# A hybrid decoder block on one core: taps at the lowest priority, one side queue per slot, LayerNorms moved into the first phase

## The chip, the cores and the metric

The kernel runs on one core of one Trainium2 chip. The metric is the time of one execution in microseconds (us) on the device. Five engines work beside each other, each in its own fixed order of instructions: PE (matrix products; its weight loads are shown as PEld), DVE (vector), ACT (scalar functions), POOL (GpSimd), and SP, which issues the transfers between device memory and SBUF. Engines wait for each other by semaphores.

## The reference

Sequence 2048, width 1024, one layer. An RMS norm with adaLN scale and shift feeds one input projection to nine groups of columns. Two branches read it:

```python
h = _rmsnorm(x, norm_g) * (1.0 + scale) + shift
p = h @ w_in            # c_val, c_gate, c_og, ts (r, k, v, two low-rank parts), r_og, g_conv, g_rwkv
# branch A
u = c_val * sigmoid(c_gate)
u = causal_depthwise_conv(u, width 31) + b
u = silu(layernorm(u)) * silu(c_og)
y_conv = u @ w_conv_out
# branch B, per head of 64, over time t
state = state * w_t - (state @ kk_t) b_t + v_t k_t ; o_t = state @ r_t
o = groupnorm(o) + sum(r * k * r_k) * v
y_rwkv = (o * silu(r_og)) @ w_rwkv_out
# merge
m = sigmoid(g_conv) * y_conv + sigmoid(g_rwkv) * y_rwkv
out = rmsnorm(x + gate * (m @ w_out)) * final_g
```

`shift`, `scale` and `gate` are three column groups of `silu(c) @ ada_w + ada_b`.

## The kernel before

**Precision and products.** Every large product is made of three: the operands are split into a high and a low part, and `mm3` (L183) adds high·high, low·high and high·low for each of eight k tiles, 24 matmuls of 128x128 by 512 columns. `load_w` (L150) brings a weight tile; the input weights are split in block 0 as they are first used and written back as two tiles (`kh_in`, `kl_in`) that later blocks read. Other weights are split ahead by `presplit` (L132), two halves for each of sixteen items of the list `later`, in blocks 1 and 2.

**First phase.** The sequence is cut into four blocks of 512 rows, and each block into four slots (`slot`, L979), one per group of four heads. A slot has 18 products: K, R and V for two pairs of heads, and the list `FILL`: two convolution columns (`c`, two products each) and two of each of the four gates. A convolution column is then 31 taps on DVE (`taps`, L856), each a pass over 128x512 from a PSUM accumulator. A pair of heads is prepared by `pair` (L483). `group` (L627) inverts the triangular blocks (POOL, L653 and L655), then runs eight chunks of 64 rows, each of three steps on PE with DVE between them, then the group norm (L803 to L812), two sets of transposes (L819) and the write of `o`.

**Order.** PE's order is that of the program text: PE is under a manual schedule. The text is interleaved by a small written clock: each matmul product adds to `now`, and tasks (generators) go on when their due time has come. `yield a, b` means that the step just issued took `a` us of PE and the next is due `b` us later. `drain` advances the clock until the named tasks are done; no product is issued meanwhile. A slot begins with a drain of its predecessor's side task and of the group opened two slots earlier; a group starts only when the group before it is done. The order on the other engines, SP's queue too, is set by a planner from priorities and estimated times; `tc.high_priority(n)` moves instructions ahead by n.

**Side work in the slots.** `xnorm` (L350) norms the row tiles of the next block and transposes them. In blocks 1 and 2 `presplit` comes ahead of it. In block 3, `z_first` (L926) and `lnorm_first` (L883) do z and the LayerNorm of block 0. At a block's start `hprep` (L389) loads the normed input and splits it. All these tiles come from one pool tag, `hx`, with seven buffers. The gate column (the third part of `ada_w`) is made after slot 0 of block 0 (L1034).

**Second phase.** For each block: `rproj` (L1094, eight products) into `mr`, `cproj` (L1080, eight products), then the output projection in four column blocks (L1186 to L1188), residual, and the final norm by row tile (`finish`, L1198), one chain of small operations for each. `osplit` (L1065) makes z of the next block from `o`, `bv` and `ro`, and `lnorm` (L1120) its LayerNorm, beside the output projection. `mr` shares its buffers with the outgoing rows `xt`. The last group's recurrence runs beside the first two projections of this phase.

Of the kernel before, what the change touches and what calls it, by code (L numbers as in the profile page):

```python
# [18 lines left out]
P = 128  # L19
# [27 lines left out]
US_MM, US_K = 0.228, 0.684  # L47


XN = ((0,), (1,), (2, 3), ())  # L50
ZN = ((0, 1, 2), (3, 4, 5), (6, 7), ())
# [15 lines left out]
def hybrid_block(ctx: ExitStack, tc: tile.TileContext, x, vecs, convk, w2a2, final_g, ada, w_in, w_co, w_ro, w_o, crow, out,  # L67
# [12 lines left out]
    def scratch(n):  # L80
        return [[dp.tile([P, TB], F32, name=f"{n}{b}_{j}", tag=f"{n}{b}_{j}") for j in range(KT)] for b in range(NB)]

    o_dram, bv_dram, ro_dram, y_dram, co_dram, gc_dram, gr_dram = [
        scratch(n) for n in ("o_d", "bv_d", "ro_d", "y_d", "co_d", "gc_d", "gr_d")]

    z_dram = [dp.tile([P, TB], F32, name=f"z_d{j}", tag=f"z_d{j}") for j in range(KT)]
    u_dram = [dp.tile([P, TB], F32, name=f"u_d{j}", tag=f"u_d{j}") for j in range(KT)]
# [42 lines left out]
    later = [("o", (cb, kh)) for cb in range(4) for kh in range(2)] + [("ro", j) for j in range(KT)]  # L130
# [215 lines left out]

    def hx(name):
        return xp.tile([P, TB], F32, name=name, tag="hx")

    def xnorm(b, tts):  # L350
        for tt in tts:
# [3 lines left out]
            for half in range(2):  # L355
                xt = hx("xt")
                nc.sync.dma_start(xt, x[t0:t0 + P, half * TB:half * TB + TB])
                nc.scalar.activation(hx("xsq"), xt, AF.Square, accum_out=ss[:, half:half + 1])
                xh.append(xt)
            vs, rs = ss[:, 2:3], ss[:, 3:4]  # L360
            nc.vector.tensor_tensor(out=vs, in0=ss[:, 0:1], in1=ss[:, 1:2], op=ALU.add)
            nc.vector.tensor_scalar(out=vs, in0=vs, scalar1=1.0 / D, scalar2=RMS_EPS, op0=ALU.mult, op1=ALU.add)
            rsqrt(rs, vs, e2, nc.vector, ss[:, 4:5])
            for kh in range(2):
                nc.vector.tensor_scalar(out=xh[kh], in0=xh[kh], scalar1=rs, scalar2=None, op0=ALU.mult)
            yield 0.0, 18.0
            for kh in range(2):
# [10 lines left out]
                yield 0.6, 3.5  # L378
# [10 lines left out]
    def hprep(b):  # L389
        h = ([], [])  # L390
        for k in range(KT):
            hf = hx("hf")
            nc.sync.dma_start(hf, xT_dram[b][:, k, :])
            hsplit(h, k, hf)
        return h
# [87 lines left out]
    def pair(G, q_, box):  # L483
# [45 lines left out]
        yield 0.0, 3.0  # L529
# [29 lines left out]
        yield 0.0, 4.5  # L559

        for c4 in range(NCH // 4):
# [13 lines left out]
            yield 1.2, 2.6  # L575
# [38 lines left out]
    def opened(b, g, h, lora):  # L614
        G = Group()
        G.b, G.g, G.h, G.lora, G.tri, G.pairs, G.wait = b, g, h, lora, 0, 0, 0.0
# [10 lines left out]
    def group(G, before):  # L627
# [60 lines left out]
        yield 0.0, 4.5  # L688
# [62 lines left out]
        for c in range(NCH):  # L751
# [11 lines left out]
            yield 0.6, 2.0  # L763
# [16 lines left out]
            yield 1.1, 2.0  # L780
# [8 lines left out]
            yield 0.6, 2.8  # L789
# [13 lines left out]
        nc.vector.tensor_reduce(out=r4(st), in_=O16, axis=AX.X, op=ALU.add)  # L803
        nc.vector.tensor_scalar(out=st, in0=st, scalar1=1.0 / 64, scalar2=None, op0=ALU.mult)
        nc.gpsimd.tensor_tensor(out=O16, in0=O16, in1=bc(st), op=ALU.subtract)
        for half in range(2):
            Dm = lt.tile([P, 8, 64], F32, name="Dm", tag="oc", bufs=OCB)
            nc.scalar.activation(Dm.rearrange("p (a b) n -> p a b n", a=2), O16[:, half * 2:half * 2 + 2], AF.Square)
            nc.vector.tensor_reduce(out=st[:, half * 8:half * 8 + 8], in_=Dm, axis=AX.X, op=ALU.add)
        nc.vector.tensor_scalar(out=st, in0=st, scalar1=1.0 / 64, scalar2=GN_EPS, op0=ALU.mult, op1=ALU.add)  # L810
        rsqrt(rs, st, lt, nc.vector)
        nc.gpsimd.tensor_tensor(out=O16, in0=O16, in1=bc(rs), op=ALU.mult)  # L812
        yield 0.5, 18.0
        for q in range(2):
# [7 lines left out]
            nc.sync.dma_start(o_dram[b][pr], oc)  # L822
            yield 0.6, 2.5
            if "o" in dbg:
                nc.sync.dma_start(dbg["o"][pr, :, b * TB:(b + 1) * TB], oc)
# [30 lines left out]
    def taps(b, j, u, before):  # L856
        if before is not None:
# [3 lines left out]
        nc.vector.tensor_scalar(out=acc, in0=u[:, HALO:], scalar1=ck[:, j, HALO:HALO + 1], scalar2=vc("conv_b", j),  # L861
                                op0=ALU.mult, op1=ALU.add)
        for i in range(HALO):
            if i % 2:
                yield 0.0, 2.0
            nc.vector.scalar_tensor_tensor(out=acc if i + 1 < HALO else yj, in0=u[:, i:i + TB],  # L866
                                           scalar=ck[:, j, i:i + 1], in1=acc, op0=ALU.mult, op1=ALU.add)
# [13 lines left out]
    ln0 = {}  # L881

    def lnorm_first(part):  # L883

        def yload(j):
            yj = hx("lny")
            nc.sync.dma_start(yj, y_dram[0][j])
            return yj

        if part == 0:  # L890
            ys = yload(0)
            for j in range(1, KT):
                nc.gpsimd.tensor_tensor(out=ys, in0=ys, in1=yload(j), op=ALU.add)
            ln0["ys"] = ys
        elif part == 1:
            ps = pl.tile([P, TB], F32, name="late", tag="late")
            nc.tensor.matmul(ps, ones, ln0["ys"], start=True, stop=True)
            ln0["mean"] = ln0["ys"]
            nc.scalar.copy(ln0["mean"], ps)
            for j in range(KT):  # L900
                yj = yload(j)
# [63 lines left out]
    def once(f):  # L965
        yield free
        f()
# [298 lines left out]
```

## Time and profile before

| | |
|---|---|
| median of 3 runs | 3078.06 us (3073.18 to 3084.1) |
| the profiled execution | 3076.14 us, span 3074.4 us |
| PE busy | 2806.0 us, 91% |
| DVE busy | 2092.9 us, 68% |
| POOL busy | 1183.6 us, 38% |
| ACT busy | 1003.0 us, 33% |
| DMA | 666.90 MB, mean 217 GB/s |
| mean granted clock of PE | 0.963 |

A row of the profile's groups names line, engine, operation, tiles written and read, count, busy time, mean duration, and the idle time of the engine just ahead of it. A row of PE's waits gives the total in us, how often, and the longest. Matmuls overlap, so one that is shown with 392 ns starts about 0.23 us after its predecessor.

### The profile page before, as it was taken

How to read it: one execution, taken by the hardware profiler on the slowest of the kernel's cores; microseconds unless marked ns; L12 is line 12 of the kernel's file. 1: busy time of each engine (PE TensorE's matmuls, PEld its weight loads, DVE VectorE, ACT ScalarE, POOL GpSimd, SP SyncE). 2: the span in 40 equal slices, each digit the busy share in tenths (PEclk: the TensorE clock that was granted, in tenths of full speed). 3: DMA queues.
4: the chain of work that ended last, by engine and by line, in shares of the span. 5: the costliest groups of instructions: out<-in, count | busy, mean ns of one | idle time of the engine just before them, and what ended most of it. 6: DMA issues, size and time to landing. Idle time of an engine off the chain costs nothing.

```text
span 3074.4 us, 50973 instructions
## 1 busy us (share of the span) xinstructions
PE 2806.0 (91%) x18640; PEld 2292.0 (75%) x18640; DVE 2092.9 (68%) x4279; ACT 1003.0 (33%) x1932; POOL 1183.6 (38%) x1742
## 2 busy tenths in 40 slices
PE   6879898986999999789999998999999999799998
PEld 5657676765877778577777777778777778588888
DVE  6857676775676766766676678677877645785633
ACT  4324343423332423242333222332423223342411
POOL 3454637343424242324243334454551315652100
PEclk9989999998999999899999999999999999899999
DMA  8775767575666674656566557665664758877665
GB/s 305 271 233 200 233 226 258 199 248 173 194 198 204 194 243 159 209 170 216 176 211 220 185 169 263 208 210 171 227 199 153 256 189 293 305 250 240 217 225 177
DMA packets 354795, 666.90 MB, mean 217 GB/s; under 512 B 134704, under 2 KB 153456, under 8 KB 354544
## 3 DMA queue, kind: packets, MB, share of 16 engines
q1 hardware_dynamic: 354544, 663.64, 64.9%
q8 instruction: 147, 2.41, 0.3%
q14 instruction: 104, 0.85, 0.1%
HBM read 483.07 MB, written 179.31 MB: 215 GB/s over the span
## 4 chain that ended last, share of the span: by engine, by line
PE 40%; DVE 15%; DMA 8%; POOL 6%; issue 4%; SPq 2%; ACT 1%; POOLq 0%; DVEq 0%; ACTq 0%
PE ps_main L180 27%; DVE acc L866 5%; PE pout L1187 2%; PE pout L1186 2%; PE pout L1188 2%; DMA w_st<-w_ro_t 1%; POOL TT L655 1%; POOL itmp L653 1%; PE aux L569 1%; DMA w_gr<-grow_d 1%; PE xo L766 1%; SPq L666 1%; PE xo L740 1%; DVE S L786 1%; PE xo L782 1%
## 5 line engine op out<-in xcount | busy, mean ns | idle before, releaser
L180 PE MATMUL ps_main<-h_hi,w_hi 128*128 128x512 f32 x2304 | 966.3, 419 | 27.1 <-ACT w_hi L163 14.5
L180 PE MATMUL ps_main<-h_hi,w_lo 128*128 128x512 f32 x2304 | 918.9, 399 | 12.4 <-DMA w_lo<-kl_in 4.8
L180 PE MATMUL ps_main<-h_lo,w_hi 128*128 128x512 f32 x2304 | 915.6, 397 | 0.2 <-DVE h_lo L385 0.2
L866 DVE SCALAR_TENSOR_TENSOR acc<-u,ck,acc 128x512 f32<-128x512 f32 x928 | 697.9, 752 | 21.0
L180 PEld LDWEIGHTS ps_main<-h_hi,w_hi 128*128 128x128 f32 x2304 | 442.5, 192 | 121.5 <-ACT w_hi L163 16.4
L180 PEld LDWEIGHTS ps_main<-h_hi,w_lo 128*128 128x128 f32 x2304 | 440.2, 191 | 120.7 <-POOL w_lo L165 7.6
L180 PEld LDWEIGHTS ps_main<-h_lo,w_hi 128*128 128x128 f32 x2304 | 442.7, 192 | 80.1 <-DVE h_lo L385 1.4
L653 POOL TENSOR_TENSOR itmp<-La,TT 128x126 f32<-128x126 f32 (+22 forms) x496 | 181.9, 367 | 156.4 <-DMA La<-dA 120.5
L786 DVE SCALAR_TENSOR_TENSOR S<-xo,pe,Se 64x64 f32<-64x64 f32 x512 | 144.7, 283 | 141.9 <-PE xo L782 129.4
L163 ACT CAST w_hi<-w_st 128x1024 fp32r<-128x1024 f32 x103 | 108.0, 1048 | 307.2 <-DMA w_st<-w_in_t 128.1
L655 POOL TENSOR_TENSOR TT<-TT,itmp 128x126 f32<-128x126 f32 (+22 forms) x496 | 190.9, 385 | 35.3
L165 POOL TENSOR_TENSOR w_lo<-w_st,w_hi 128x1024 fp32r<-128x1024 f32 x50 | 120.5, 2409 | 133.0 <-ACT w_hi L163 58.2
L761 ACT ACTIVATE Se<-S,pe 128x128 f32<-128x128 f32 x256 | 89.0, 395 | 142.9 <-DVE S L786 141.9
L766 PEld LDWEIGHTS xo<-Xz,As 128*64 128x64 f32 x1024 | 69.6, 138 | 70.4 <-DVE Xz L762 38.4
L165 DVE TENSOR_TENSOR w_lo<-w_st,w_hi 128x1024 fp32r<-128x1024 f32 x53 | 70.5, 1331 | 68.0 <-PE ps_main L180 38.3
L572 DVE TENSOR_TENSOR As<-aux,maskA 128x512 f32<-128x512 f32 x128 | 82.7, 684 | 47.5 <-PE aux L569 47.0
L450 ACT ACTIVATE t<-ps_main,mu 128x512 f32<-128x512 f32 x96 | 65.9, 686 | 136.5 <-PE ps_main L180 133.9
L735 ACT COPY Xz<-xo 64x256 f32<-64x256 f32 x128 | 46.9, 367 | 189.4 <-PE xo L740 129.6
L766 PE MATMUL xo<-Xz,As 128*64 128x64 f32 x1024 | 87.4, 229 | 23.2 <-DVE Xz L762 23.0
L777 DVE TENSOR_TENSOR uv<-xo,rn 64x256 f32<-64x256 f32 x128 | 53.7, 419 | 80.3 <-PE xo L766 66.6
L847 POOL COPY u<-tail 128x30 f32<-128x30 f32 x32 | 10.2, 322 | 251.5 <-DVE yj L866 237.7
L762 DVE TENSOR_TENSOR Xz<-xo,Xz 64x256 f32<-64x256 f32 x128 | 53.7, 420 | 77.4 <-PE xo L757 75.8
(296 smaller groups left out, 5531.1 us busy)
## 6 DMA issues: line engine op xcount, KB each, us to landing
w_hi<-kh_in SPq DMA_DIRECT2D x219, 512.0 KB, 3.9
w_lo<-kl_in SPq DMA_DIRECT2D x219, 512.0 KB, 5.1
w_st<-w_in_t SPq DMA_DIRECT2D x73, 512.0 KB, 4.5
kh_in<-w_hi SPq DMA_DIRECT2D x71, 512.0 KB, 2.9
kl_in<-w_lo SPq DMA_DIRECT2D x71, 512.0 KB, 3.5
w_hi<-kh_ro SPq DMA_DIRECT2D x32, 512.0 KB, 4.0
w_lo<-kl_ro SPq DMA_DIRECT2D x32, 512.0 KB, 5.1
w_st<-w_co_t SPq DMA_DIRECT2D x32, 512.0 KB, 3.6
```

The costliest lines, as they stand in the source:

```text
L163: nc.scalar.copy(hi, st)
L165: lo_eng.tensor_tensor(out=lo, in0=st, in1=hi.bitcast(F32), op=ALU.subtract)
L180: nc.tensor.matmul(ps[:, qs], ww[:, k, :], aa[k][:, qs], start=(k == 0 and t == 0 and q == 0), stop=(k == KT - 1 and t == 2 and q == ms - ...
L450: nc.scalar.activation(t1, ps, AF.Identity, scale=mu1[:, mi:mi + 1])
L572: nc.vector.tensor_tensor(out=Asb[:, hh, c4 * 4:c4 * 4 + 4, :].rearrange("p (a e) n -> p a (e n)", e=2), in0=pA[hh], in1=flat(maskA).unsqu ...
L653: nc.gpsimd.tensor_tensor(out=tmp[:, :ni, :nt], in0=La[:, j:j + 1, j + 1:].broadcast_to([P, ni, nt]), in1=TT[:, :ni, j:j + 1].broadcast_to ...
L655: nc.gpsimd.tensor_tensor(out=TT[:, :ni, j + 1:], in0=TT[:, :ni, j + 1:], in1=tmp[:, :ni, :nt], op=ALU.add)
L761: nc.scalar.mul(Se[:, q, :], Sg[:, q, :], R[q]["pe"][:, c:c + 1])
L766: nc.tensor.matmul(b_[pr_, q, hs], As[q][:, hh, c, kcol(e)], Xz[:, e, q, hs], start=(n == 0), stop=(n == 3), skip_group_check=True)
L786: nc.vector.scalar_tensor_tensor(out=Sg[hs, q, hs], in0=b_[hs, 2 + q, hs], scalar=R[q]["pe"][hs, c:c + 1], in1=Se[hs, q, hs], op0=ALU.mult ...
L866: nc.vector.scalar_tensor_tensor(out=acc if i + 1 < HALO else yj, in0=u[:, i:i + TB], scalar=ck[:, j, i:i + 1], in1=acc, op0=ALU.mult, op1 ...
L1186: nc.tensor.matmul(o_, mhi[kk][:, ts_], whi[:, k, :], start=first, stop=False, skip_group_check=True)
```

## The change

1. The taps carry a priority of −1500, below everything else.
2. Each slot has one side task, `sides(b, g)`: the norm of the next block (row tiles 0 and 1 in slot 0, 2 and 3 in slot 1), then the gate column (slot 0 of block 1), then steps of the LayerNorm of block b−1 (slots 1 to 3 of blocks 1 to 3), then the weight splits of blocks 1 and 2. The list `later` has the `ro` weights first.
3. `lnorm_first` is a generator for any of blocks 0 to 2, and the second phase only loads and splits its result. z is made in the tail of each group, by two POOL operations on each pair, instead of in `z_first` and `osplit`. Block 3 keeps `lnorm` in the second phase.
4. The loads of the next block's input are issued ahead of the last three products of a block.
5. Small operations of the block norm and the group norm get a high priority; many due times are longer. The final norm's small operations are one chain for four row tiles, except in the last column block of the last block.

```diff
+LOWP = 1500
-XN = ((0,), (1,), (2, 3), ())
-ZN = ((0, 1, 2), (3, 4, 5), (6, 7), ())
+XN = ((0, 1), (2, 3), (), ())
...
-    later = [("o", (cb, kh)) for cb in range(4) for kh in range(2)] + [("ro", j) for j in range(KT)]
+    later = [("ro", j) for j in range(KT)] + [("o", (cb, kh)) for cb in range(4) for kh in range(2)]
...
     def xnorm(b, tts):
+        held = []
         for tt in tts:
...
-            yield 0.0, 18.0
+            held.append((tt, xh))
+            yield 0.0, 8.0
+        yield 0.0, 28.0
+        for tt, xh in held:
             for kh in range(2):
...
+    def hload(b):
+        hfs = []
+        for k in range(KT):
+            hf = hx("hf") if k < HXB else e1.tile([P, TB], F32, name="hf", tag="sq")
+            nc.sync.dma_start(hf, xT_dram[b][:, k, :])
+            hfs.append(hf)
+        return hfs
...
@@ def pair @@
-        yield 0.0, 3.0
+        yield 0.0, 4.5
-        yield 0.0, 4.5
+        yield 0.0, 6.0
-            yield 1.2, 2.6
+            yield 1.2, 3.0
@@ def group @@
-        yield 0.0, 4.5
+        yield 0.0, 6.0
-            yield 0.6, 2.0
+            yield 0.6, 2.6
-            yield 1.1, 2.0
+            yield 1.1, 2.5
-            yield 0.6, 2.8
+            yield 0.6, 3.3
...
-        yield 0.5, 18.0
+        yield 0.5, 30.0
+        yield lambda: G.gated
         for q in range(2):
...
-            nc.sync.dma_start(o_dram[b][pr], oc)
+            for src, op in ((bv_dram, ALU.add), (ro_dram, ALU.mult)):
+                zt = spare("zt")
+                nc.sync.dma_start(zt, src[b][pr])
+                nc.gpsimd.tensor_tensor(out=oc, in0=oc, in1=zt, op=op)
+            nc.sync.dma_start(z_dram[b][pr], oc)
             yield 0.6, 2.5
...
+            with tc.high_priority(-LOWP):
+                nc.vector.scalar_tensor_tensor(out=acc if i + 1 < HALO else yj, in0=u[:, i:i + TB],
+                                               scalar=ck[:, j, i:i + 1], in1=acc, op0=ALU.mult, op1=ALU.add)
...
+    def sides(b, g):
+        if b + 1 < NB:
+            yield from xnorm(b + 1, XN[g])
+        if b == 1 and g == 0:
+            yield from gate_col()
+        yield from norms(b, g)
+        if b in (1, 2):
+            for _ in range(2):
+                n_ = later.pop(0)
+                for half in range(2):
+                    presplit(*n_, half)
+                    yield 0.0, 4.0
+    def norms(b, g):
+        if b and g >= 1:
+            t = lns.setdefault(b, lnorm_first(b - 1))
+            for _ in range((0, 3, 5, 99)[g]):
+                r = next(t, None)
+                if r is None:
+                    break
+                yield r
...
+        fill(len(todo) - 3)
+        drain(*side)
+        hfs = hload(b + 1)
         fill(len(todo))
+        return hfs
...
-            ohl = osplit(b + 1)
-            uhl = lnorm(b + 1)
+            ohl = lsplit(z_dram[b + 1], okt(b + 1))
+            uhl = lsplit(u_dram[b + 1], utiles()) if b + 2 < NB else lnorm(b + 1)
...
+            def tail_rs(tt, n):
+                vs = f2.tile([P, n], F32, name="vs", tag=f"vs{n}")
+                nc.vector.tensor_reduce(out=vs, in_=sq4[:, tt:tt + n, :], axis=AX.X, op=ALU.add)
+                nc.vector.tensor_scalar(out=vs, in0=vs, scalar1=1.0 / D, scalar2=RMS_EPS, op0=ALU.mult, op1=ALU.add)
+                rs = f2.tile([P, n], F32, name="rs2", tag=f"rs{n}")
+                rsqrt(rs, vs, f2, nc.vector, f2.tile([P, n], F32, name="rs_t", tag=f"rt{n}"))
+                return rs
...
         if b + 1 < NB:
+            rall = tail_rs(0, NTT)
             for tt in range(NTT):
-                finish(tt)
+                finish(tt, rall)
```

`gate_col` makes the gate column from sixteen loads of 128x512 with one DVE operation each, 3 us apart by the written clock. `lnorm_first(b)` loads y three times (for the mean, the variance and the output), does its sums and products on POOL (46 operations), squares and the swish on ACT and DVE, and writes `u_dram[b]`.

245 lines of the change are left out of this document (120 added, 125 removed).

## The prediction

> **What bounds the kernel now.** I read the page first, then the engines by stage, then what TensorE (PE) waited for, then single places.
>
> ```profile
> span 3074.4 us, 50973 instructions
> ...
> PE 2806.0 (91%) x18640; PEld 2292.0 (75%) x18640; DVE 2092.9 (68%) x4279; ACT 1003.0 (33%) x1932; POOL 1183.6 (38%) x1742
> ```
> PE is the bound, and it sits idle for 3074.4 − 2806.0 = 268 us. No edit takes a large matmul away, so the change can only win or lose in those 268 us and in the clock that PE loses behind them. The profiled execution took 3076.14 us, 1.9 us under the median of 3078.06; all sums start from 3076.
>
> The stretches below are blocks 0 to 3 of the first phase, then the first two projections of the second phase, then its middle. Columns: length, busy time of PE, PEld, DVE, ACT, POOL, granted clock, DMA share.
> ```profile
> 0.00:663.00 663.00, 571.87 (x3573) 453.24 (x3573) 478.23 (x963) 259.46 (x447) 322.62 (x433) 0.94 0.71 239
> 663.00:1262.00 599.00, 551.51 (x3882) 446.46 (x3880) 407.08 (x883) 191.17 (x390) 222.31 (x396) 0.97 0.62 199
> 1262.00:1866.00 604.00, 557.36 (x3881) 451.22 (x3880) 417.10 (x893) 190.59 (x390) 202.42 (x380) 0.96 0.60 194
> 1866.00:2437.00 571.00, 544.72 (x3831) 439.89 (x3831) 421.14 (x842) 177.98 (x343) 260.24 (x417) 0.99 0.63 210
> 2437.00:2562.00 125.00, 116.49 (x772) 93.25 (x773) 69.67 (x136) 33.70 (x65) 17.82 (x12) 0.95 0.62 206
> 2617.00:2880.00 263.00, 230.12 (x1139) 192.25 (x1139) 194.52 (x323) 96.56 (x162) 121.46 (x78) 0.94 0.74 254
> ```
> Block 3 already carries a LayerNorm and the z products in its slots, has no norm of a next block, and is the shortest block: 571 us against 599 and 604.
>
> PE's waits (total, times, longest), the rows the sum uses:
> ```profile
> PE late L371 <- DVE xt L365: 49.4, 2, 27.7
> PE xo L766 <- DVE Xz L762: 23.0, 22, 3.0
> PE ps_main L180 <- DVE mr L1100: 18.5, 2, 15.9
> ...
> PE ps_main L180 <- ACT h_hi L384: 12.2, 3, 5.3
> ...
> PE aux L533 <- ACT sq L525: 9.9, 7, 4.7
> ...
> PE aux L569 <- POOL KR L552: 6.8, 5, 2.3
> PE xo L782 <- DVE uv L777: 6.7, 7, 3.7
> ...
> PE ps_main L180 <- DMA w_lo<-kl_in: 4.8, 3, 2.3
> PE aux L589 <- DVE As L572: 4.6, 5, 1.6
> ...
> PE xo L757 <- DVE S L786: 3.9, 5, 1.3
> ...
> PE pmean L1132 <- POOL ys L1130: 2.0, 1, 2.0
> ```
>
> **Price of the clock.** After the 27.7 us wait PE ran like this:
> ```profile
> 716.00:721.00 5.00, 4.93 (x14) 4.10 (x15) 0.32 (x1) 1.51 (x4) 0.00 (x0) 0.50 0.32 105
> ```
> Half clock for 5 us: a long wait costs 5 × 0.5 = 2.5 us on top of itself. I charge that for every long wait that goes or comes.
>
> **The change, part by part.**
>
> *The block norm goes ahead of the weight splits (gain 54).* In blocks 1 and 2, slot 0 first issues four halves of weight splits, and the norm's loads come behind them on SP, in the same seven `hx` buffers:
> ```profile
> 672.79 0.54 SPq L139 DMA_DIRECT2D w_st<-w_o_t  x1
> ...
> 694.42 0.41 SPq L142 DMA_DIRECT2D w_gr<-grow_d  x1
> ...
> 700.70 0.42 SPq L357 DMA_DIRECT2D xt<-x_in  x1
> ...
> 702.09 0.38 SPq L357 DMA_DIRECT2D xt<-x_in  x1
> ```
> The loads go out 28 us after the first split, while the transposes are due after 18 us; PE, whose order is fixed, stands. In the new side queue the norm is first and its transposes are due 8+28 us after the second tile's loads. I take both waits as gone: 49.4 + 2 × 2.5 = 54 (from 0, if another user of `hx` delays them, to 54). Late next would be the splits, on which nothing in the block waits.
>
> *Group norm tail (gain 18).* It rises in priority and gets 30 us instead of 18 before its transposes. In block 0 its wait is the second largest:
> ```profile
> PE late L819 <- POOL uv L812: 17.6, 2, 10.9
> ```
> With two clock losses that is 22.6; I take 18, between 0 and 22.6. Its z products (two POOL operations per pair, two more loads) stand behind the transposes, and PE waits for none of them before the second phase.
>
> *Gate column from block 0 to block 1 (gain 9).* Eight 512 KB loads on SP and eight DVE operations leave block 0, where weights are still being split as they are used; from 140 to 215 us PE waited:
> ```profile
> PE ps_main L180 <- ACT w_hi L163: 14.0, 3, 5.9
> PE ps_main L180 <- POOL w_lo L165: 3.7, 3, 1.4
> ```
> Part of this is block 0's own weight traffic; I take half of 17.7, bounds 0 and 18. In block 1 the same bytes come as sixteen loads spaced by 3 us.
>
> *Loads of the next block's input (gain 12).* They go out three products early instead of at the boundary. Three waits of 12.2 with 7.5 of clock; the split still needs the old block's `h_hi` buffers back, which the last product holds, so I keep 12 of 19.7 (bounds 0, 20).
>
> *Second phase without the LayerNorms of blocks 1 and 2 (gain 28).* The last-named wait of `mr` (15.9) is a queue on DVE: four separate chains of tiny operations, final scale, then `mr`, whose buffer is that of the outgoing `xt`.
> ```profile
> 2621.72 9.95 POOL L1151 TENSOR_TENSOR y<-y,rl 128x512 f32<-128x512 f32 x8 [1.95 <-DVE rs_t L112]
> ...
> 2626.81 1.28 DVE L114 SCALAR_TENSOR_TENSOR rs<-rs_t,rs 128x1 f32<-128x1 f32 x2
> ...
> 2642.22 0.23 DVE L114 SCALAR_TENSOR_TENSOR rs<-rs_t,rs 128x1 f32<-128x1 f32 x2
> ...
> PE ps_main L180 <- DVE w_lo L165: 6.3, 3, 5.7
> ```
> Beside LayerNorm's POOL work two one-column operations took 1.28 us, without it 0.23. One joined chain, and no LayerNorm there, should leave about 2 us of output DMA: 14 + 2.5; the `w_lo` wait goes, 5.7 + 2.5; `pmean` 2.0; the second `mr` wait (18.5 − 15.9 = 2.6) loses 1. Sum 27.7; bounds 8 and 30. Block 3's LayerNorm stays, and so does the end: the last row tiles keep their own small chains.
>
> *Taps lowest, longer due times (gain 20).* The waits for Xz, uv, S, KR, As and sq come to 23.0+6.7+3.9+6.8+4.6+9.9 = 55. Taps no longer stand ahead of those operations on DVE and each step has 0.4 to 1.5 us more cover. How the planner really orders DVE the trace cannot show; between 0 (or below: taps late would hold `u`) and 55 I take 20.
>
> *The price of longer due times: the chain of groups (cost 15).* A group's steps, here in slot 6 of the run, which PE's `pw` row delimits (981.7 to 1121.0):
> ```profile
> L495 PE MATMUL aux<-lw,wl x3: 388/388/477, 981.7 to 1121.0; 128*128 128x512 f32 x3
> ...
> L700 PE MATMUL late<-T,As x32: 191/191/212, 991.8 to 992.8; 32*32 32x32 f32 x32
> ...
> L740 PE MATMUL xo<-uv,As x64: 222/222/270, 1015.9 to 1085.5; 128*64 128x64 f32 x64
> ...
> L819 PE MATMUL late<-ident,uv x8: 270/272/273, 1104.3 to 1107.8; 128*128 128x128 f32 x8
> ...
> 1085.74 0.37 ACT L744 COPY uv<-xo 64x256 f32<-64x256 f32 x1 [1.97 <-PE xo L740]
> ...
> L812 POOL TENSOR_TENSOR uv<-uv,grs x1: 1906/1906/1906, 1096.1 to 1096.1; 128x1024 f32<-128x1024 f32 x1
> ```
> Start 991.8, last output 1085.5, transposes 1104.3 and 1107.8, done near 1111: 10 us before the slot ends. The next slot drains this group first, and the next group may not start before it is done. The change adds 8 × (0.6+0.5+0.5) = 12.8 to the chunks, 12 to the tail and 1.5 at the start: 26, so each group overruns its 139 us slot; starting right behind its predecessor (about 8 us in) it needs 8 + 94 + 12.8 + 31 + 6 = 152, some 12 over. The drain then steps the written clock without products. Of the 12 the last 6 are the transposes' own steps, so the tail keeps 31 − 6 = 25 us of cover, and its real length is 1085.7 to 1098.0, 12.3 us. So PE should not stand for the tail; but the two sets of transposes come back to back through one PSUM buffer, and the second waits for the copy out of the first:
> ```profile
> L821 ACT ACTIVATE oc<-late,hgb,hgg x32: 773/780/782, 353.3 to 2564.9; 128x512 f32<-128x512 f32 x32
> ```
> 0.78 plus hand-over, say 1.1 us, in 14 slots: 15 (bounds 0, and 14 × 12 = 168 if the lag is paid in full).
>
> *The last group (cost 22).* Before, its transposes came at 2560, where the sixteen products of the 125 us stage end. It now starts some 12 us later and takes 26 longer, so 36 us of written time lie behind the products: the last 1.4 chunks (about 4.5 us each by the operations in them, 6), the tail 12.3, the transposes 2, and 2.5 of clock: 22. Bounds 0 and 40.
>
> *Moved work (cost 10).* Two LayerNorms (46 POOL operations each) and z of three blocks (48) at about 1.3 us:
> ```profile
> L902 POOL TENSOR_TENSOR lny<-lny 128x512 f32<-128x512 f32 x8 | 10.1, 1293 | 0.1
> ```
> 140 × 1.3 = 182 us of POOL in the first phase, some 60 in each of blocks 1 and 2, up to block 3's 260. Block 3 shows that much hidden; I charge 5.
> [...]
> Their y, gate and z transfers join the weight loads on SP: the 4.8 of `w_lo<-kl_in` doubles, 5. Bounds 0 and 40.
>
> Sum: gains 54+18+9+12+28+20 = 141, costs 15+22+10 = 47, net 94: **2982 us**.
>
> **Rivals.**
> *A, slower: the chain of groups becomes the bound.* If the drain's lag is real waiting, 12 us plus 2.5 of clock in 14 slots are 203 in place of my 15: 2982 + 188 = 3170. It decides from (141 − 32)/14 = 7.8 us a slot. For it: the arithmetic of the written clock. Against: a step's real latency, 12.3 in the tail, is well under its cover.
>
> *B, POOL's work returns as DVE waits.* The row at 2626.81 is the mechanism: two-input DVE operations stretch while POOL streams. If the moved 182 us double the waits for Xz, uv and S (33.6) and the gain of 20 is lost, 2982 + 54 = 3036. Against: block 3, with that POOL load, waits no more than block 2.
> [...]
>
> *C, the small waits nearly all go.* 45 instead of 20, hprep and block 0 at their upper ends (+18), the last group half: 2982 − 54 = 2928.
>
> *D, no effect:* `hx` is short again and the norm waits as before, while the costs come: −87 + 47 leaves 3036 with the norm alone lost; no change at all needs phase 2 lost too. Little speaks for it.
>
> **Chances.** My forecast 0.50 (own range 2950 to 3015), C 0.16, B and D with time won 0.19, unchanged 0.03, A 0.12. Runs lay between 3073 and 3084, so 0.3% (9 us) is about what can be told. Range 2910 to 3060: it leaves out A and the edges of C.
>
> **What would show it.** Right: the `late L371` row gone from PE's waits, blocks 1 and 2 near 575 us, the stretch with `mr` near 235 instead of 263, and one wait of 15 to 20 us for `uv L812` at the end of the second projection. A wait for L812 or L821 at every slot's start would be A; longer DVE rows in blocks 1 to 3 with Xz waits above 23 would be B.

## The result and the profile after

The changed kernel took 3032.14 us (median of 4 runs, 3025.17 to 3034.97), the kernel before on the same chip 3077.48: 0.9847 of the time, 95% interval 0.9822 to 0.9873. It is faster, by 45 us; 94 were forecast. The profiled execution took 3034.01 us.

The page's first part, of the kernel after:

```profile
span 3032.2 us, 51026 instructions
...
PE 2817.1 (93%) x18640; PEld 2297.6 (76%) x18640; DVE 2072.0 (68%) x4160; ACT 1001.3 (33%) x1936; POOL 1229.8 (41%) x1790
```
PE now stands idle for 3032.2 − 2817.1 = 215 us, 53 fewer than before. But the same 18640 instructions kept it busy for 11 us more.

To see where, both spans are cut at the starts of the same four products: blocks 0 to 3 of the first phase, then the second phase. Columns as in the prediction: length, busy time of PE, PEld, DVE, ACT and POOL, granted clock, DMA share, GB/s. Before:

```profile
0.00:667.50 667.50, 573.73 (x3577) 454.27 (x3578) 481.62 (x971) 260.08 (x448) 322.62 (x433) 0.94 0.71 240
667.50:1269.20 601.70, 551.56 (x3881) 446.55 (x3880) 407.62 (x885) 191.17 (x390) 222.31 (x396) 0.97 0.62 199
1269.20:1872.00 602.80, 557.19 (x3881) 451.21 (x3880) 416.20 (x890) 190.59 (x390) 202.42 (x380) 0.96 0.61 195
1872.00:2437.80 565.80, 542.99 (x3829) 438.77 (x3827) 418.85 (x837) 178.16 (x344) 260.24 (x417) 0.99 0.63 208
2437.80:3074.40 636.60, 580.55 (x3476) 501.21 (x3476) 368.61 (x700) 183.01 (x361) 176.05 (x116) 0.96 0.70 239
```
After:

```profile
0.00:651.60 651.60, 568.15 (x3577) 452.84 (x3577) 475.99 (x939) 259.12 (x448) 329.62 (x439) 0.95 0.72 243
651.60:1268.00 616.40, 570.42 (x3888) 457.67 (x3885) 456.01 (x951) 208.16 (x418) 285.67 (x442) 0.96 0.68 222
1268.00:1868.70 600.70, 565.70 (x3888) 453.54 (x3885) 437.40 (x909) 206.03 (x416) 304.64 (x458) 0.97 0.68 223
1868.70:2438.00 569.30, 547.12 (x3831) 440.67 (x3828) 419.27 (x850) 177.32 (x344) 263.74 (x421) 0.99 0.61 201
2438.00:3032.20 594.20, 565.72 (x3468) 492.86 (x3468) 283.37 (x516) 150.63 (x313) 46.17 (x31) 0.98 0.68 229
```
The first phase ends where it ended, at 2438. All of the gain, 636.6 − 594.2 = 42.4 us, is in the second phase. By phases my terms had said the reverse: 88 of the 94 in the first. Block 0 won 15.9, block 1 lost 14.7, with 63 us more of POOL and 48 more of DVE in it.

What PE waited for, after (total, times, longest):

```profile
PE late L839 <- POOL uv L831: 23.3, 4, 16.1
PE xo L784 <- DVE Xz L780: 20.8, 14, 3.8
PE ps_x L439 <- DVE dg L431: 18.2, 2, 17.1
PE ps_main L179 <- DMA w_hi<-kh_in: 15.1, 3, 5.8
PE late L839 <- ACT oc L841: 14.4, 15, 1.1
PE ps_main L179 <- DVE mr L1144: 9.8, 5, 6.5
...
PE late L722 <- DVE Qs L728: 9.1, 8, 1.9
PE late L718 <- DVE T L705: 7.9, 2, 4.6
```
The norm's wait for `xt` (49.4) and the one for `h_hi` (12.2) are gone; `w_hi<-kh_in` and the transposes' `oc` came. The sum of idle time fell in every block, yet the first phase is as long as before: idle fell from 212.3 to 186.6 there, and PE's busy time rose from 2225.5 to 2251.4. What was won in waits came back as 26 us of longer busy time. By the trace's clock record, half clock took 66 us out of PE's busy time in the first phase, against 51 before, which is 15 of the 26; the products of the moved norms are in the rest.

### The profile page after: what moved, and what is told of

It reads as the page before. It is cut to its first block, busy times and chain, and to the rows that moved or that the text cites. A ratio compares the mean times of both kernels' runs of the same rounds, so it can differ in the third digit from the quotient of the medians.

```text
span 3032.2 us, 51026 instructions
## 1 busy us (share of the span) xinstructions
PE 2817.1 (93%) x18640; PEld 2297.6 (76%) x18640; DVE 2072.0 (68%) x4160; ACT 1001.3 (33%) x1936; POOL 1229.8 (41%) x1790
## 5 line engine op out<-in xcount | busy, mean ns | idle before, releaser
L179 PE MATMUL ps_main<-h_hi,w_hi 128*128 128x512 f32 x2304 | 970.6, 421 | 19.7 <-DMA w_hi<-kh_in 15.1
L890 DVE SCALAR_TENSOR_TENSOR acc<-u,ck,acc 128x512 f32<-128x512 f32 x928 | 696.7, 751 | 15.9
L780 DVE TENSOR_TENSOR Xz<-xo,Xz 64x256 f32<-64x256 f32 x128 | 53.5, 418 | 86.0 <-PE xo L775 78.9
L845 POOL TENSOR_TENSOR oc<-oc,zt 128x512 f32<-128x512 f32 x64 | 81.7, 1285 | 66.6 <-ACT oc L841 39.6
L784 PE MATMUL xo<-Xz,As 128*64 128x64 f32 x1024 | 87.9, 230 | 20.9 <-DVE Xz L780 20.8
L587 PE MATMUL aux<-KR,BK 64*128 64x128 f32 x1024 | 82.2, 291 | 17.8 <-DVE As L590 9.3
```

Of the source, the lines that this page charges most:

```text
L179: nc.tensor.matmul(ps[:, qs], ww[:, k, :], aa[k][:, qs], start=(k == 0 and t == 0 and q == 0), stop=(k == KT - 1 and t == 2 and q == ms - ...
L587: nc.tensor.matmul(pA[hh][:, c // 2, es], BK[hs, cc, es], KR[hs, cc, es], start=(c == 0), stop=(c == 3), skip_group_check=True)
L784: nc.tensor.matmul(b_[pr_, q, hs], As[q][:, hh, c, kcol(e)], Xz[:, e, q, hs], start=(n == 0), stop=(n == 3), skip_group_check=True)
L845: nc.gpsimd.tensor_tensor(out=oc, in0=oc, in1=zt, op=op)
```

## The experiments

Each kernel was timed beside the kernel before on the same chip; ratios are to that, with 95% intervals. Stage times come from one profile each; block 1 took 614.1 to 616.4 us in the four kernels that keep both the column and the norm in it (the changed one and the runs on the taps, on the second PSUM buffer and on the column's write). Edits also let the planner order DVE anew, so a single part moves a block by some us either way, and the parts' prices do not add up exactly.

**First question: is it the moved LayerNorms, the due times, the taps or the joined norm?**

LayerNorm of blocks 1 and 2 back in the second phase, the rest as changed:
```diff
-        if b and g >= 1:
-            t = lns.setdefault(b, lnorm_first(b - 1))
+        if b == 3 and g >= 1:
+            t = lns.setdefault(b, lnorm_first(0))
...
-            uhl = lsplit(u_dram[b + 1], utiles()) if b + 2 < NB else lnorm(b + 1)
+            uhl = lnorm(b + 1)
```


> The changed kernel with the LayerNorms of blocks 1 and 2 back in the second phase (block 0's stays in block 3's slots, as before the change). Moved-work theory: the LayerNorm work in blocks 1 and 2 is what ate the gains of the first phase; the first phase (2438 us in the changed kernel) shortens by 25 to 45 us, the second (594) grows by 25 to 40, the total stays within 3015 to 3045. Chain theory: the due times are at fault; the first phase stays within 10 us of 2438, only the second grows, total 3055 to 3075.

Measured: 3025.51 us, 0.983 (0.9807 to 0.9852). The windows of block 1 and of the second phase:
```profile
651.60:1248.60 597.00, 559.88 (x3881) 451.31 (x3880) 431.20 (x932) 190.91 (x393) 224.99 (x396) 0.97 0.65 211
...
2414.70:3026.60 611.90, 576.65 (x3476) 498.42 (x3476) 346.64 (x586) 182.91 (x361) 114.51 (x75) 0.97 0.67 229
```
Block 1 falls from 616.4 to 597.0, the first phase from 2438.0 to 2414.7; the second phase rises by 17.7. The move costs 23 where it goes to and gains 18 where it comes from, both less than the 25 us or more that were expected. The total, 7 us, is within the spread of the two kernels' runs; that the move gains nothing is what can be said.

The due times of before:
```diff
-        yield 0.0, 4.5
+        yield 0.0, 3.0
...
-        yield 0.5, 30.0
+        yield 0.5, 18.0
```
(and six more between them, each back to the value of before)

> The changed kernel with the eight due times of pair, group and group norm as they were before the change. Chain theory: groups end inside their slots again, the 14.4 us of waits of the transposes for the copy of the first set (15 times) vanish, half-clock stretches go down, first phase 20 to 40 us shorter, total 2990 to 3012. Moved-work theory: with more work on DVE and POOL the shorter due times are not met; waits for Xz, uv, S and the group norm grow by 20 us or more, total 3030 to 3070.

Measured: 3071.03 us, 0.9975 (0.9962 to 0.9988). PE's waits, and the window of the second phase:
```profile
PE xo L784 <- DVE Xz L780: 25.3, 24, 4.0
...
PE ps_main L179 <- DVE mr L1144: 15.1, 3, 13.6
PE late L718 <- DVE T L705: 13.6, 2, 10.5
```
```profile
2459.80:3072.50 612.70, 568.58 (x3468) 495.83 (x3468) 288.15 (x522) 149.56 (x313) 40.52 (x28) 0.96 0.66 222
```
Without the longer due times 39 us of the 45 are lost, some in every stage: the waits for Xz come 24 times instead of 14, those for `mr` and `T` rise from 9.8 and 7.9 to 15.1 and 13.6. Nearly half of it, 18.5 us, is lost in the second phase, where only the last group still runs by these times; how they act there is not shown. The chain's own cost did show: the transposes' wait for `oc`, 14.4 in the changed kernel, is 1.0 here. It is smaller than what the cover saves. So the longer times are no net cost; rival A falls, and so does my net of 20 − 15 − 22.

The taps at normal priority:
```diff
-LOWP = 1500
+LOWP = 0
```


> The changed kernel with the taps at the normal priority. If the low priority gave the 20 us of my sum: waits for Xz, uv, S, As and KR grow by 15 to 25 us and the total is 3045 to 3060. If it gave nothing: 3025 to 3040. If it harms (the order is worse): below 3025.

Measured: 3036.58 us, 0.986 (0.9832 to 0.9888), first phase 2439.4. The taps' priority is worth nothing that can be told (0 to 4 us).

The joined chain of the final norm alone, in the kernel before:
```diff
-            def finish(tt):
+            def tail_rs(tt, n):
...
+            def finish(tt, rall=None):
...
+            rall = tail_rs(0, NTT)
             for tt in range(NTT):
-                finish(tt)
+                finish(tt, rall)
```


> The kernel before with the final norm's small operations joined and nothing else. If the four separate chains were what mr waited for in the second phase: the 15.9 us wait falls to 8 or less, the total is 3062 to 3070. If it was POOL's LayerNorm beside them: the wait stays above 12 and the total within 5 us of 3077.

Measured: 3083.25 us, 1.0015 (1.0004 to 1.0027): no gain, and the wait stays:
```profile
PE ps_main L180 <- DVE mr L1100: 22.8, 3, 17.4
```

**Second question: what is each moved part worth?**

The norm ahead of the splits alone, in the kernel before:
```diff
+    def sides(b, g):
+        yield from xnorm(b + 1, XN[g])
+        if b in (1, 2):
+            for _ in range(2):
+                n_ = later.pop(0)
+                for half in range(2):
+                    presplit(*n_, half)
+                    yield 0.0, 4.0
...
-            side[:] = [Task(xnorm(b + 1, XN[g]))]
+            side[:] = [Task(sides(b, g))]
```


> The kernel before, with the weight splits put behind the block norm in one side task per slot, nothing else. My step: both waits for xt (49.4 us and 5 of clock) go and nothing takes their place: total 3020 to 3030. Rival: the splits, now later, hold the hx buffers and SP against something else, and half or more comes back as other waits: total 3045 to 3075.

Measured: 3044.3 us, 0.9891 (0.9867 to 0.9914). Blocks 1 and 2, then PE's waits in them:
```profile
666.70:1252.70 586.00, 554.69 (x3882) 448.75 (x3881) 406.68 (x886) 190.67 (x390) 223.35 (x396) 0.98 0.63 204
1252.70:1838.60 585.90, 553.87 (x3881) 448.31 (x3880) 414.05 (x890) 190.12 (x390) 203.51 (x380) 0.98 0.61 200
```
```profile
PE aux L533 <- ACT sq L525: 12.8, 6, 4.7
PE late L371 <- DVE xt L365: 10.4, 2, 5.9
```
This one edit gives 33 us, three quarters of what the whole change gives, and lies between the two ranges expected. The `xt` wait falls from 49.4 to 10.4. Its transposes still come due after the 18 us of before, and the four half splits are now 4 us apart; both are part of this edit's result.

The gate column back behind slot 0 of block 0, in one piece:
```diff
-        if b == 1 and g == 0:
-            yield from gate_col()
...
+                if b == 0 and g == GG:
+                    for _ in ada_cols(srow, l3, "As", ASB, ...):
+                        pass
...
+                    nc.sync.dma_start(grow_d.rearrange("(n p) -> p n", p=P), hgate_col)
```


> The changed kernel with the gate column back behind slot 0 of block 0. If the move gained in block 0 as I had it (9 us) and cost nothing in block 1: total 3035 to 3045. If the move only carried the wait from block 0 to block 1 (there a weight load stands on SP behind the write of the gate column, 5.8 us and half clock after it): block 0 longer and block 1 (616 us) shorter by about the same 8 to 15 us, total 3022 to 3037.

Measured: 3017.18 us, 0.9804 (0.9781 to 0.9827). Block 0 and block 1:
```profile
0.00:658.00 658.00, 569.82 (x3575) 453.04 (x3576) 484.74 (x957) 259.88 (x448) 328.36 (x439) 0.95 0.74 247
658.00:1251.10 593.10, 560.19 (x3887) 452.06 (x3886) 439.57 (x912) 206.72 (x416) 285.04 (x442) 0.98 0.67 223
```
Moving the column had won 6.4 us in block 0 and lost 23.3 in block 1: a loss of 17 by stages (15 by the medians) where I had a gain of 9. The total is below both ranges expected.

The second set of transposes in another PSUM buffer:
```diff
-            po = pl.tile([P, NTT, P], F32, name="late", tag="late")
+            po = (pl, pa)[q].tile([P, NTT, P], F32, name=("late", "aux")[q], tag=("late", "aux")[q])
```


> The changed kernel with the second set of a group's transposes in one of the two aux PSUM buffers instead of the one the first set is copied from. If the 14.4 us of waits for that copy, and half-clock stretches behind them, are a cost of the longer chain: they go, total 3010 to 3022. If the drain merely finds the next wait (aux taken from the next pair): total 3026 to 3040.

Measured: 3023.16 us, 0.9829 (0.9801 to 0.9858); first phase 2437.0. The row `late L839 <- ACT oc L841` (14.4) is gone, and `late L722 <- DVE Qs L728` went from 9.1 to 17.5. In this execution the stages did not move: what the drain does not spend here it spends at the next step. But it is the slowest of the four (3034.67; the others 3019.62 to 3025.8). By the medians the kernel is 9 us faster than the changed one, with intervals that overlap, so a small gain is neither shown nor excluded.

z made as before (`z_first`, `osplit`):
```diff
-            for src, op in ((bv_dram, ALU.add), (ro_dram, ALU.mult)):
-                ...
-            nc.sync.dma_start(z_dram[b][pr], oc)
+            nc.sync.dma_start(o_dram[b][pr], oc)
...
-            ohl = lsplit(z_dram[b + 1], okt(b + 1))
+            ohl = osplit(b + 1)
```


> The changed kernel with z made as before (block 0 in block 3's slots, the others in the second phase) instead of in each group's tail. If moving z is what shortened the second phase beyond the LayerNorm: the second phase grows from 594 by 12 to 25 us while the first shortens by 5 to 15, total 3032 to 3050. If z's place does not matter: both within 5 us of the changed kernel's, total 3025 to 3037.

Measured: 3040.46 us, 0.9883 (0.9858 to 0.9908): first phase 2419.8, second 610.2, with the `mr` wait at 16.5 instead of 9.8. By this profile z's move cost 18 and gained 16. The profiled execution, though, is the fastest of the four (3031.84), 9 us under their median; by the medians the move is worth a gain of 8 us, with intervals that overlap. The 18 may be too large by as much.

**Third question: what in the moved LayerNorm costs the time, its transfers or its arithmetic?** Two kernels put part of it into blocks 1 and 2. One keeps only the transfers, so LayerNorm of blocks 0 and 1 isn't computed; the other adds all 46 POOL operations, and leaves out the squares, the root, the activation and the two products of the sums on PE.
```diff
-            t = lns.setdefault(b, lnorm_first(b - 1))
+            t = lns.setdefault(b, (lnorm_first if b == 3 else lnorm_moves)(b - 1))
...
+        for j in range(KT):
+            yj = yload(j)
+            ct = hx("lnc")
+            nc.sync.dma_start(ct, co_dram[b][j])
+            nc.sync.dma_start(u_dram[b][j], yj)
+            yield 0.0, 6.0
```


> The changed kernel with the LayerNorms of blocks 0 and 1 (slots of blocks 1 and 2) reduced to their transfers: y is loaded three times, the gate once, and y is stored in place of the result; the sums, squares, swish and the two products are left out. With the LayerNorms in place blocks 1 and 2 take 616 and 601 us, without them 597 and 594. If the transfers and their place on SP are the cost: 610 to 617 and 598 to 602. If the arithmetic on POOL, DVE and ACT is: 594 to 601 and 591 to 596.

In the second kernel the sums and differences ahead of this loop are back on POOL, and the loop has:
```diff
             yj = yload(j)
+            nc.gpsimd.tensor_tensor(out=yj, in0=yj, in1=ys, op=ALU.subtract)
+            nc.gpsimd.tensor_tensor(out=yj, in0=yj, in1=qs, op=ALU.mult)
             ct = hx("lnc")
             nc.sync.dma_start(ct, co_dram[b][j])
+            nc.gpsimd.tensor_tensor(out=yj, in0=yj, in1=ct, op=ALU.mult)
```


> The changed kernel with the LayerNorms of blocks 0 and 1 (slots of blocks 1 and 2) reduced to their transfers and their POOL operations; squares, rsqrt, swish and the two products are left out. Transfers alone gave 598 us for block 1, all of it 616. If POOL's work is the cost (it stretches DVE operations and delays POOL's own part of the pairs): block 1 at 610 to 617. If the ACT, DVE and PE part is: 596 to 602.

Measured: transfers alone 3018.43 us (0.9799, 0.9782 to 0.9817), with POOL's work 3046.89 (0.99, 0.9882 to 0.9919). Block 1, transfers alone:
```profile
651.00:1248.80 597.80, 559.82 (x3884) 453.03 (x3882) 431.39 (x932) 191.13 (x393) 225.85 (x396) 0.97 0.69 228
```
and with POOL's work, block 1 and then PE's longest wait in it:
```profile
649.00:1272.50 623.50, 566.47 (x3884) 456.84 (x3882) 442.54 (x932) 191.45 (x393) 281.31 (x442) 0.95 0.67 218
```
```profile
PE late L718 <- DVE T L705: 17.6, 2, 12.6
```
With the transfers block 1 is as long as without any LayerNorm (597.8 against 597.0), at 228 GB/s; the whole norm makes it 616.4. So its arithmetic costs the time there, not its transfers.

That it is POOL's share of the arithmetic is not shown. With 55 us more of POOL block 1 is 26 us longer, but that is more than the whole norm costs, and by a way that the changed kernel does not take. `T` is made from what POOL's triangular steps leave. The 62 of them for the second group of block 1 span 53.4 us in this kernel, with 26.2 us of other POOL work between them; with the transfers alone they span 31.2 us, and in the changed kernel 30.8, each with 3.4 us of other work. The kernel with POOL's part has no squares on ACT between the norm's POOL operations, and these land elsewhere. PE's waits in block 1 of the changed kernel, then of the run without the moved norms:
```profile
PE xo L784 <- DVE Xz L780: 9.8, 5, 3.8
PE late L718 <- DVE T L705: 4.6, 1, 4.6
```
```profile
PE xo L784 <- DVE Xz L780: 5.7, 4, 2.6
PE late L718 <- DVE T L705: 5.0, 1, 5.0
```
The wait for `T` is the same with the norm and without. Of the norm's 19.4 us in block 1, 8.9 are idle time of PE, with Xz and `w_hi<-kh_in` up by some 4 each; 10.5 are longer busy time, of which 8 are half clock. Which of the norm's operations bring this about stays open. In block 2 the transfers alone gave 603.7, more than the whole norm's 600.7 (594.3 without it); there the parts can't be told apart.

**Fourth question: does the column cost by its place?** The column in small steps in slot 2 of block 0, and that with the LayerNorms back:
```diff
-        if b == 1 and g == 0:
+        if b == 0 and g == 2:
             yield from gate_col()
```


> The changed kernel with the gate column, made in the same small steps, in slot 2 of block 0, where the side queue is empty. If what hurts in block 1 is a heap of side work in one slot (norm, gate column, splits): block 1 falls to 590 to 597 us as with the column behind slot 0, and block 0 stays at 651 to 656; total 3005 to 3016. If the column costs its 15 us wherever it stands: block 0 rises to 660 or more, total 3020 to 3032.

> The same, and the LayerNorms of blocks 1 and 2 back in the second phase. If both effects add: first phase 2395 to 2405, second 610 to 615, total 3000 to 3015, the fastest so far. If the gate column's cost came from the LayerNorm's neighbourhood: total no better than 3020.

Measured: 3023.01 us (0.9809, 0.9791 to 0.9828) and 3015.23 (0.9783, 0.9761 to 0.9804). In the first, block 1 falls to 593.1 as with the column behind slot 0, but block 0 rises from 651.6 to 668.1. In this form the column costs 16.5 us in block 0 and 23.3 in block 1; in one piece behind slot 0 it cost 6.4. In the second the two effects add: 9 and 7 us alone, 17 together, with 2405.4 for the first phase and 610.9 for the second. The column's last step writes 1024 single elements to `grow_d`, and SP's queue stood behind that write for 8 us in the changed kernel. So the write was issued from ACT:
```diff
-        nc.sync.dma_start(grow_d.rearrange("(n p) -> p n", p=P), hgate_col)
+        nc.scalar.dma_start(grow_d.rearrange("(n p) -> p n", p=P), hgate_col)
```


> The changed kernel with the one write of the finished gate column issued from ACT instead of SP. If this write, which a weight load on SP waited 8 us for, is the column's cost in block 1: block 1 falls from 616 to 600 to 606 us, the wait for w_hi near 771 us goes, total 3015 to 3025. If the sixteen loads and DVE operations are: block 1 at 611 to 618, total 3025 to 3037.

Measured: 3035.49 us (0.9862, 0.9839 to 0.9886), block 1 615.9: no gain. SP's waits, first in the changed kernel, then with the write on ACT:
```profile
SPq L155 <- DMA grow_d<-hgate_col: 8.0, 1, 8.0
```
```profile
SPq L138 <- DMA grow_d<-hgate_col: 9.5, 1, 9.5
```
SP stood behind the write all the same, with a weight split's load, so this run did not take the cause away. Whether the write, the sixteen loads or the sixteen DVE products cost the 23 us stays open.

**Fifth question: are the longer due times a gain by themselves?** They were put alone into the kernel before:
```diff
-        yield 0.0, 3.0
+        yield 0.0, 4.5
...
-        yield 0.5, 18.0
+        yield 0.5, 30.0
```


> The kernel before with the eight longer due times and nothing else. If longer due times gain by themselves (shorter waits at each step outweigh the longer chain): total 3040 to 3065. If they pay only where the slots carry more work, the 39 us that they were worth in the changed kernel do not show: total 3070 to 3095.

Measured: 3069.3 us, 0.9973 (0.996 to 0.9987): 7 us, against 39 in the changed kernel, and between the two ranges expected. In its profile (of the slowest of ten executions, 3077.81) blocks 1 and 2 are 19 us shorter than in the kernel before, block 0 12.5 and block 3 7 us longer, and the second phase is as before (637.2 against 636.6). The transposes' wait for `oc`, 0.9 before, is 18.2 here. So part of the cover's worth comes only together with the rest of the change. That the load on POOL and DVE is the reason is not shown: nearly half of the 39 lies in the second phase, where both have less to do than before.

**A version from these runs:** the change without its two losing parts, with the gate column as before and the LayerNorms of blocks 1 and 2 in the second phase (the edits of the first and the sixth run together).

> The changed kernel with the LayerNorms of blocks 1 and 2 back in the second phase and the gate column back behind slot 0 of block 0. If the two add: blocks 658, 571, 594, 571, second phase 611: total 3000 to 3010, faster than both kernels and than every run so far. If not: 3012 to 3020, as with either alone.

Measured: 3007.54 us (2998.59 to 3018.85), 0.9774 (0.9745 to 0.9804), under both kernels. From the run with the column behind slot 0 (0.9781 to 0.9827) and the one with the column in slot 2 and the LayerNorms back (0.9761 to 0.9804) it can't be told apart. Blocks 0 to 2, in the fastest of its four executions (2998.59):
```profile
0.00:657.70 657.70, 570.20 (x3577) 453.32 (x3577) 486.20 (x957) 259.34 (x448) 328.49 (x439) 0.95 0.74 247
657.70:1230.50 572.80, 553.48 (x3883) 447.03 (x3881) 413.24 (x893) 189.83 (x391) 223.51 (x396) 0.99 0.65 212
1230.50:1817.60 587.10, 556.23 (x3884) 448.81 (x3881) 416.32 (x890) 189.63 (x391) 243.72 (x412) 0.98 0.64 210
```
Block 1 comes to 572.8, near the 575 that the prediction expected of the change itself, once the two moved loads are out of it; block 2 comes to 587.1.

## Why the prediction was right and wrong

The direction and the range held; 2982 was too low by 50 us, and the first phase was misjudged by 88. The step that failed is **Moved work (cost 10)**: "Block 3 shows that much hidden; I charge 5." Measured, the LayerNorms cost 23 us in the first phase and z up to 18. With it failed the gate column, which I had booked as a gain of 9: it cost 15 to 17 net. Together these are some 55 us, more than the 49 by which the gain fell short. Block 3 was the wrong row to go by: it has no weight splits and no norm of a next block, so it says nothing of blocks 1 and 2, which have both. By the step's own numbers these two came above block 3's 260 us of POOL, too: 222 and 202, plus 60 for the norm and 21 for z, are 303 and 283; 286 and 305 were measured. That the weight splits or the next block's norm are what makes the difference was not tried.

That 3032 still lies in the range is luck in part: the norm and the group norm tail fell short by 21 and 18 us as well, and the longer due times, for which I had charged 15 and 22, were a gain on the whole.

Put together for the first phase from the runs: the norm's order −29 (2409.0 with it alone, against 2437.8), due times −22 (2438.0 against 2459.8), LayerNorm +23, column +17, z +18. The sum is +7; measured 0. For the second: LayerNorm −18, z −16, due times −18 (612.7 to 594.2) make −52; measured −42. The wait for `mr` is 5 to 7 us longer both in the run on z and in the run on the due times, so some of it may be counted twice. All of these are stage times of one profile each, z's with the margin named above.

Of the four signs named for the forecast, two came: the `late L371` row is gone, and the stretch with `mr` is shorter (see below). Blocks 1 and 2 did not fall to 575, and no wait for `uv` stands at the end of the second projection.

Step by step:

- *Block norm ahead (54):* the mechanism was right, the size was not. Alone it gave 33, with 10.4 us of the wait left and the `sq` waits up.
- *Group norm tail (18):* failed. The wait is 23.3 after 18.3. The wait of 16.1 lies in block 0; DVE in the last 7 us of it, in the timeline of the kernel after (start, duration):

```profile
340.95 0.76 DVE L890 SCALAR_TENSOR_TENSOR acc<-u,ck,acc 128x512 f32<-128x512 f32 x1
341.61 2.22 DVE L112 SCALAR_TENSOR_TENSOR rs_t<-rs_t,gst 128x16 f32<-128x16 f32 x1
343.75 0.73 DVE L890 SCALAR_TENSOR_TENSOR yj<-u,ck,acc 128x512 f32<-128x512 f32 x1
344.41 0.16 DVE L113 SCALAR_TENSOR_TENSOR grs<-rs_t,grs 128x16 f32<-128x16 f32 x1
...
344.82 0.17 DVE L112 SCALAR_TENSOR_TENSOR rs_t<-rs_t,gst 128x16 f32<-128x16 f32 x1
```
  The taps (0.76 each) still stand between the tail's small operations, at the lowest priority too. And the 30 us of cover were not there: PE's last product before the wait ends at 331.8, and the drain steps through the rest of the due time without products. With the short due times the longest of these waits is 8.0 (changed kernel) and 10.9 (kernel before), with the long ones 16.1 and 15.7. This is rival A's mechanism, at this one place.
- *Gate column (9):* wrong in sign, see above.
- *Early loads (12):* the `h_hi` wait went, but `w_hi<-kh_in`, which is no row of before's waits, now takes 15.1. Its longest wait (5.8) is for the load that SP's queue held back behind the column's write; the other two end at 1222.6 and 1823.3, some 45 us before a block's end. The early loads are not what they stand behind. SP at the first of them:

```profile
1216.66 0.61 SPq L155 DMA_DIRECT2D w_hi<-kh_in  x1
...
1218.96 0.46 SPq L405 DMA_DIRECT2D hf<-xT  x1
```
  The first early load (`hf`) goes out behind the weight's load, which itself stands behind write-backs of weight splits and stores of `bv` and the gates. No run took this part of the change away, so its own worth is not known.
- *Second phase without LayerNorm (28):* the phase won 42, but not in the way I had it. The norms' return costs 18; z's (16) and the due times' (18) were not counted there. The wait for `mr`, which was to give 16.5, does not hang on the LayerNorm: it is 4.6 with both norms back and 16.5 with z back, and the joined chain alone left it at 22.8. From the first product of block 1's `rproj` to that of block 2's `cproj` it took 218.6 us before (from 2616.8) and takes 191.5 now (from 2607.2): 27 less, as forecast.
- *Taps and due times (20):* taps 0; due times 7 alone and 39 in the changed kernel.
- *Chain of groups (15):* the wait between the two sets of transposes came as priced, 14.4 in 15 at up to 1.1 us. Taking it away gave 9 us by the medians and nothing in the one profile, so whether it is a cost of its own is open.
- *The last group (22):* did not come. No row for `uv L831` stands in the second phase; the output projection's products ran between the last chunk and the transposes:

```profile
2556.24 0.68 PE L758 MATMUL xo<-uv,As 128*64 128x64 f32 x8
...
2557.64 0.28 PE L1235 MATMUL pout<-w_hi,o_lo 128*128 128x256 f32 x1
```
  PE's order is not fixed by the text in that stage; I had assumed that it was. The trace of before had it already: output products (L1186) run from 2562.04 on, between the last group's two sets of transposes at 2560.20 and 2564.16.
- *Rival B* named 3036, and 3032 was measured. That the number is so near is chance. Xz waits as a whole fell to 20.8, although in block 1 the norm raised them from 5.7 to 9.8, and the operations that PE waits for there did not stretch beside POOL (0.427 us against 0.418, last section). The time came back through the arithmetic of the norms, z, the gate column and the clock; that POOL's part of the arithmetic is the cause is not shown.

## What to carry to other kernels

Idle time of an engine in another phase was not free room here: the LayerNorms cost 23 us where they went and saved 18 where they came from. So price moved work by a run in the block that it goes to, and not by a block that lacks that block's other work. Longer due times in a hand-written order were worth 7 us alone and 39 together with the load: try such cover with the load, and judge it by taking it out again. Test each part of a mixed change alone: one reordering gave 33 of the 45 us here, and two parts gained nothing or lost, under which a faster kernel lay. Look at which of its executions a profile shows before its stages are compared.

## What the hardware showed that was not expected

**Small vector operations lasted until the GpSimd instruction beside them ended.** In the fence above, a 128x16 operation takes 2.22 us at 341.61, where the same line takes 0.17 at 344.82. Beside it, on POOL:
```profile
341.46 2.34 POOL L164 TENSOR_TENSOR w_lo<-w_st,w_hi 128x1024 fp32r<-128x1024 f32 x1 [7.70 <-ACT w_hi L162]
```
Both end at 343.8. It is no single case: thirteen of the small steps of the two norms' roots (tiles 128x1 and 128x16, two inputs in SBUF) take over 0.6 us in this trace, and each ends within 0.05 us of the end of a POOL operation beside it. The rows show the times; what makes the operation wait they do not show. Grouped over block 1, the two-input L597 took 687 ns on average without the moved LayerNorm, 791 with it, and 940 in the kernel with POOL's part alone. Two kinds of operation with one input in PSUM were not held up: the Xz additions (L780) that began during a POOL operation with two inputs have a median of 0.427 us, the others 0.418, and none took over 0.429; for the taps the median is 0.755 in both cases, and none took over 0.758.

**Half clock after a 2 us wait.** No long wait stood ahead of this clock loss. At 751.8 PE had waited 1.94 us for `Xz`; the windows ahead of it, right behind it and after:
```profile
742.00:747.00 5.00, 4.82 (x32) 3.58 (x31) 4.91 (x15) 1.05 (x3) 0.00 (x0) 1.00 0.72 210
752.50:755.90 3.40, 3.40 (x17) 2.90 (x16) 3.34 (x7) 2.20 (x5) 1.13 (x1) 0.50 0.15 34
756.00:761.00 5.00, 4.99 (x26) 3.90 (x26) 2.73 (x10) 1.61 (x5) 0.11 (x1) 1.00 0.35 68
```
From the trace's clock record, block 1 lost 22 us of PE's busy time in ten such stretches, against 7 us in four before: 15 of the 19 us by which PE's busy time rose there. My price of 2.5 us "for every long wait" left the short ones out.

In these traces the sum of idle time goes with the half clock, not the single wait. The clock record of this trace starts 28.9 us into the span. All its 33 half-clock stretches begin on one grid of 3.41 us, and all but the last, which the span's end cuts, last one to five such pieces. Of the pieces at full clock in which PE was idle for 1.9 us or more, all 24 are followed by half clock; of those with 1.6 to 1.9 us, 5 of 8; of the 793 with less, 4. The trace of before gives 25 of 25, 5 of 8 and 0 of 793. The piece from 957.3 on has 1.98 us of idle time, in waits of 1.11 and 0.87, and two pieces at half clock follow it. The wait of 2.58 us that ends at 689.3 falls into two pieces, 0.91 and 1.67, and none follows. So two waits of about 1 us inside one piece cost more clock here than one of 2.58 across two.
